# A fourth summed pair in the last gate/up block of a Hymba layer, with down's first activations split in steps of their own and the weight buffers handed out otherwise

## The chip, the cores and the metric

The kernel runs on one core of a Trainium2 chip. The metric is device microseconds of one execution, taken as the median of several runs. A profile of one execution comes with it. In it PE is the matrix engine (TensorE), PEld its weight load, DVE the vector engine, ACT the scalar engine, POOL is GpSimd and SP the engine that here only issues DMAs. All times are in microseconds unless ns is written.

## What is computed

The reference is one decoder layer on 256 tokens with a model width of 2048, all of it in 32-bit floats:

```
u = rmsnorm(h) ; [lru_x|lru_gate|q|k|v|ret_gate] = u @ W_in      # 2048 -> 6144
a = rg_lru(causal_conv(lru_x)) * gelu(lru_gate)                  # gated linear recurrence
b = groupnorm(retention(rope(q), rope(k), v)) * silu(ret_gate)   # 8 heads of 128, chunks of 128
h = h + concat(a, b) @ W_out                                     # 2048 -> 2048
t = rmsnorm(h) ; h = h + (silu(t @ W_gate) * (t @ W_up)) @ W_down  # 2048 -> 5632 -> 2048
out = rmsnorm(h)
```

Nearly all the work is in the products with W_in, W_out, W_gate, W_up and W_down.

## The kernel before

**Three products for one.** The matrix engine multiplies in a rounded 32-bit format (fp32r). Every operand is therefore kept as a rounded high part and a low rest, made by `split`: ACT casts the high part (line 123) and DVE subtracts it from the source (line 124). One product of two blocks is three matmuls, high by high, high by low and low by high (`three`, lines 683 to 685).

**Path of a weight.** SP issues a DMA of 128 x 1024 floats (512 KB) into a `raw` buffer, ACT casts it into a `wh` tile, DVE subtracts into a `wl` tile, and PE reads both. There are 6 raw buffers (`rpool`) and 4 pairs of split tiles (`wpool`). From block 3 on, where the tiles of the mixer are no longer needed, `swap` opens two pools more: 2 raw buffers (`raw2`) and 2 pairs of split tiles (`split2`), and every fourth raw tile and every third split tile comes from them. `stop_more` ends that before block 12, and `swap_back`, after block 12, closes the two pools and puts in their place the tiles of the end: the residual `htok` (8 DMAs of 256 KB on POOL's queue) and the final norm's weights `fw` (4 more of 256 KB).

**Blocks and steps.** After the mixer the program consists of blocks: 0 and 1 (W_out), 2 to 12 (gate and up, 512 columns of each in a block, `NB` = 11) and two passes of down (`down_block`). A block goes through 8 pairs of 128-row slices of its weights (2 x 2 blocks of 128 x 512 for one pair). A plain pair takes 8 products, which are 24 matmuls. A summed pair takes 7, by sums of weight blocks and of activation blocks, which are 21 matmuls; for it DVE makes 4 sums of 128 x 512 (`add`, line 661), more pieces are split, and the second half of the weights is loaded a second time. A summed pair is worked off in two places: 4 of its products in the block before its own (`share`, class `Shared`), the other 3 in its own (`direct`, class `Direct`, with the second load). `SUMMED` says which pairs of a block are summed, and `STEPS` writes a block's steps as letters: p a plain pair, h half of one, s a share of the next block's summed pair, d a direct step. Blocks 4 to 10 have the steps `psdhsdhsdhsdhp`. The last three shares, in block 12, are those of down's first three pairs.

**Order.** A list of entries (weights to load, function to run) is walked in order; at each entry the loads are issued 3 ahead of need (`AHEAD`), and `tick` runs what was put off by `defer`. The framework's scheduler then sets the order of instructions on each engine, and adds the waits between engines and for free buffers.

**Other names that the change touches.** `sumsq` (line 291) collects the sum of squares of x for the first norm: ACT squares (line 308), POOL adds seven times (line 310) and folds once (line 311), and PE sums over the partitions (`rms_scale`, line 271). `make_left(p)` splits activation tile `ff[p]` for down, with its sums. `ft` (line 865) are the transposes of a gate/up block's result and `ff` (line 867) ACT's copies of them out of PSUM. `cr` and `sr` are tables for the rotation.

Of the kernel before, what the change touches and what calls it, by code (L numbers as in the profile page):

```python
# [8 lines left out]
F32 = mybir.dt.float32  # L9
# [5 lines left out]
P = 128  # L15
D = 2048
S = 256
# [14 lines left out]
SUMMED = ((), (4, 5), (2, 3), (1, 2, 3)) + ((0, 1, 2, 3),) * 8 + ((1, 2, 3),)  # L32
# [3 lines left out]
STEPS = ("pppspppspp", "ppspdpsdpp", "pdpsdpspspp", "pspsdpsdpsdp") + ("psdhsdhsdhsdhp",) * 7 + ("psdpsdpsddp", "psdpsdpsdpp")  # L36


EARLY_DOWN = (0, 1, 2)
SUMMED_DOWN = (9, 12, 15, 17, 19), (5, 7, 9, 11, 13, 15, 17)  # L40
# [4 lines left out]
def tile_hymba_layer(ctx: ExitStack, tc: tile.TileContext, A: dict, out: bass.AP):  # L45
# [5 lines left out]
    rpool = ctx.enter_context(tc.tile_pool(name="raw", bufs=6))  # L51
# [5 lines left out]
    late, resid, more, turn_of = [], [xpool], [], [0, 0]  # L57
# [16 lines left out]
    def split_tiles():  # L74
        turn_of[1] += 1
        pool_ = more[1] if more and turn_of[1] % 3 == 0 else wpool
        return [pool_.tile([P, 1024], F32R, tag=g, name=nm(g)) for g in ("wh", "wl")]

    def raw_tile():
        turn_of[0] += 1  # L80
        pool_ = more[0] if more and turn_of[0] % 4 == 0 else rpool
        return pool_.tile([P, 1024], F32, tag="raw", name=nm("raw"))
# [76 lines left out]
    program = []  # L159
# [131 lines left out]
    sumsq = cpool.tile([P, 512], F32, name="sumsq")  # L291
# [148 lines left out]
    cr = cpool.tile([P, S], F32, name="cr")  # L440
    sr = cpool.tile([P, S], F32, name="sr")
# [15 lines left out]
    half = {}  # L457
# [159 lines left out]
    class Quad:  # L617
# [5 lines left out]
        def __init__(self, src, sums, before=None):  # L623
            self.src, self.sums, self.before = src, sums, before
            self.parts = {}
            self.apart = False
# [12 lines left out]
        def load(self, half):  # L639
            r = raw_tile()  # L640
            nc.sync.dma_start(out=r, in_=self.src[:, half * 1024 : half * 1024 + 1024])
            if half == 0 and self.before:
                self.before()
            if not self.sums:
                self.cut(("b22", "b21") if half else ("b11", "b12"), r)
                return
            if half == 0:
                self.ra = r
                self.parts["b11"] = act_tile("bh", F32R), act_tile("bl", F32R)
                split(*self.parts["b11"], r[:, :512])  # L650
                return
            self.cut(("b22", "b21"), r)
            self.add(r)
            self.cut(("t1", "t3"), self.ra)
            self.cut(("t2", "t4"), r)
# [31 lines left out]
    def block(index, quads, lefts, post, ps, tail, early={}, ordered=False):  # L687
# [39 lines left out]
        for i in range(n):  # L727
            program.append(([quads[i]], step(i)))

# [30 lines left out]
    class Direct(Quad):  # L760
# [8 lines left out]
        def load(self, half):  # L769
            r = raw_tile()  # L770
            nc.sync.dma_start(out=r, in_=self.src[:, 1024:2048])
            self.cut(("b22", "b21"), r)
            self.parts["t4"] = self.shared.parts["t4"]
# [12 lines left out]
    class Block:  # L786
# [45 lines left out]
        def put(self, after):  # L832
            plain = [i for i in PLAIN[self.index] if i not in self.summed]
            for k, kind in enumerate(self.steps):
                if kind == "p":
                    i, n = plain.pop(0), len(plain)
                    quad = Quad(self.src(i), False)
                    run = lambda i=i, quad=quad, k=k, n=n: self.plain(i, quad, k == 0, n == 0)
# [12 lines left out]
                else:  # L851
                    m = self.steps[:k].count("s")
                    quad = after.shared[m]
                    run = lambda m=m: after.share(m)
                program.append(([quad], run))
# [258 lines left out]

    blocks = [Block(d, lambda i, d=d: A["w_out"][8 * d + i], y, out_post(d), STEPS[d], SUMMED[d]) for d in range(2)]
    blocks += [
# [4 lines left out]
    for b, after in zip(blocks, blocks[1:] + [down]):  # L1121
        if b.index == 3:
            program.append(([], swap))
        if b.index == NB + 1:
            program.append(([], stop_more))
        b.put(after)
    program.append(([], swap_back))
# [120 lines left out]
```

## Time and profile before

| | |
|---|---|
| runs, median (lowest to highest) | 1082.09 us (1081.95 to 1083.99) |
| profiled execution | 1082.46 us, of which the span is 1080.7 us |
| PE busy | 1070.2 us, 99% of the span |
| DVE, ACT, POOL busy | 964.1 us (89%), 664.5 us (61%), 57.2 us (5%) |
| granted TensorE clock | 0.998 of full |
| read from HBM | 239.46 MB, 225 GB/s over the span with what is written |

The busy shares stand per engine over the whole span. The chain of work that ended last is followed back from the last instruction, each piece to what released it; it is PE for 98%, and 22% each is one of the three lines of `three`. A view of waits lists, for an engine, how long it sat idle just before instructions of a line, and what ended that.

### The profile page before, as it was taken

How to read it: one execution, taken by the hardware profiler on the slowest of the kernel's cores; microseconds unless marked ns; L12 is line 12 of the kernel's file. 1: busy time of each engine (PE TensorE's matmuls, PEld its weight loads, DVE VectorE, ACT ScalarE, POOL GpSimd, SP SyncE). 2: the span in 40 equal slices, each digit the busy share in tenths (PEclk: the TensorE clock that was granted, in tenths of full speed). 3: DMA queues.
4: the chain of work that ended last, by engine and by line, in shares of the span. 5: the costliest groups of instructions: out<-in, count | busy, mean ns of one | idle time of the engine just before them, and what ended most of it. 6: DMA issues, size and time to landing. Idle time of an engine off the chain costs nothing.

```text
span 1080.7 us, 14590 instructions
## 1 busy us (share of the span) xinstructions
PE 1070.2 (99%) x5089; PEld 897.7 (83%) x5089; DVE 964.1 (89%) x1399; ACT 664.5 (61%) x947; POOL 57.2 (5%) x73
## 2 busy tenths in 40 slices
PE   9999999999999999999999999999999999999997
PEld 7888888888888888888888888888888888888886
DVE  7889789988878889989999999999999889997886
ACT  7666644468756676656656565665656656654563
POOL 0602230000000000000000000000002000000001
PEclk9999999999999999999999999999999999999999
DMA  9965475554556588677776777777767856474662
GB/s 325 336 213 171 159 254 166 183 176 158 192 195 234 183 304 273 231 235 256 257 270 228 251 260 242 263 269 232 258 234 270 289 181 214 162 245 159 214 212 101
DMA packets 71386, 244.62 MB, mean 226 GB/s; under 512 B 8208, under 2 KB 8592, under 8 KB 71312
## 3 DMA queue, kind: packets, MB, share of 16 engines
q1 hardware_dynamic: 68400, 236.34, 64.6%
q0 software_dynamic: 1472, 4.72, 1.3%
q10 hardware_dynamic: 1440, 2.62, 0.6%
q8 instruction: 40, 0.66, 0.2%
q14 instruction: 34, 0.28, 0.1%
HBM read 239.46 MB, written 4.19 MB: 225 GB/s over the span
## 4 chain that ended last, share of the span: by engine, by line
PE 98%; DVE 1%; DMA 1%; POOL 0%; SPq 0%; ACT 0%; issue 0%; POOLq 0%; ACTq 0%
PE c L685 22%; PE c L683 22%; PE c L684 22%; PE fm L194 11%; PE fm L196 5%; PE tm L174 3%; PE tm L175 3%; PE tm L176 3%; PE p L683 1%; PE p L685 1%; PE p L684 1%; PE ft L865 1%; DMA x<-in_x 1%; PE ht L588 0%; PE sc L492 0%; DVE wl L124 0%
## 5 line engine op out<-in xcount | busy, mean ns | idle before, releaser
L123 ACT CAST wh<-raw 128x1024 fp32r<-128x1024 f32 (+1 forms) x498 | 462.9, 959 | 323.8 <-PE c L685 130.8
L124 DVE TENSOR_TENSOR wl<-raw,wh 128x1024 fp32r<-128x1024 f32 (+1 forms) x498 | 542.2, 1115 | 72.5 <-ACT wh L123 71.2
L684 PE MATMUL c<-wl,ah 128*128 128x512 f32 x826 | 322.7, 391 | 0.0
L685 PE MATMUL c<-wh,al 128*128 128x512 f32 x826 | 321.8, 390 | 0.0
L683 PE MATMUL c<-wh,ah 128*128 128x512 f32 x826 | 280.3, 391 | 0.0
L683 PEld LDWEIGHTS c<-wh,ah 128*128 128x128 f32 x826 | 155.1, 188 | 32.0 <-ACT wh L123 0.3
L685 PEld LDWEIGHTS c<-wh,al 128*128 128x128 f32 x826 | 155.2, 188 | 31.8
L684 PEld LDWEIGHTS c<-wl,ah 128*128 128x128 f32 x826 | 155.2, 188 | 31.6
L194 PE MATMUL fm<-u,wh 128*128 128x512 f32 x512 | 161.4, 396 | 0.0
L196 PEld LDWEIGHTS fm<-u,wl 128*128 128x128 f32 x512 | 96.1, 188 | 22.4
L196 PE MATMUL fm<-u,wl 128*128 128x256 f32 x512 | 101.2, 279 | 0.0
L661 DVE TENSOR_TENSOR raw<-raw,raw 128x512 f32<-128x512 f32 x114 | 78.4, 689 | 2.0
L661 DVE TENSOR_TENSOR raw<-raw 128x512 f32<-128x512 f32 x114 | 78.3, 688 | 1.4
L194 PEld LDWEIGHTS fm<-u,wh 128*128 128x128 f32 x512 | 78.4, 189 | 0.3
L684 PE MATMUL c<-wl,sh 128*128 128x512 f32 x192 | 74.3, 390 | 0.0
L685 PE MATMUL c<-wh,sl 128*128 128x512 f32 x192 | 73.7, 390 | 0.0
L683 PE MATMUL c<-wh,sh 128*128 128x512 f32 x192 | 67.3, 391 | 0.3 <-ACT sh L123 0.3
L176 PE MATMUL tm<-wh,u 128*128 128x512 f32 x128 | 48.7, 391 | 0.0
L175 PE MATMUL tm<-wl,u 128*128 128x512 f32 x128 | 48.7, 393 | 0.0
L174 PE MATMUL tm<-wh,u 128*128 128x512 f32 x128 | 46.9, 394 | 1.4 <-ACT u L298 1.4
L683 PEld LDWEIGHTS c<-wh,sh 128*128 128x128 f32 x192 | 36.1, 188 | 8.1 <-ACT sh L123 0.7
L685 PEld LDWEIGHTS c<-wh,sl 128*128 128x128 f32 x192 | 36.1, 188 | 7.5
(247 smaller groups left out, 1027.4 us busy)
## 6 DMA issues: line engine op xcount, KB each, us to landing
raw<-in_w_gu SPq DMA_DIRECT2D x216, 512.0 KB, 5.3
raw<-in_w_down SPq DMA_DIRECT2D x91, 512.0 KB, 4.6
raw<-in_w_out SPq DMA_DIRECT2D x34, 512.0 KB, 3.7
raw<-in_w_lx SPq DMA_DIRECT2D x16, 512.0 KB, 6.4
raw<-in_w_k SPq DMA_DIRECT2D x16, 512.0 KB, 3.6
raw<-in_w_q SPq DMA_DIRECT2D x16, 512.0 KB, 4.2
raw<-in_w_rg SPq DMA_DIRECT2D x16, 512.0 KB, 3.5
raw<-in_w_lg SPq DMA_DIRECT2D x16, 512.0 KB, 3.5
```

Of the source, the lines that this page charges most:

```text
L123: act.copy(out=dst_h, in_=src)
L124: v.tensor_tensor(out=dst_l, in0=src, in1=dst_h.bitcast(F32), op=ALU.subtract)
L174: pe.matmul(ps, ah, wh, start=first, stop=False)
L175: pe.matmul(ps, ah, wl, start=False, stop=False)
L176: pe.matmul(ps, al, wh, start=False, stop=last)
L194: pe.matmul(ps, wh, hl, start=n + i == 0, stop=False)
L196: pe.matmul(ps[:, :S], wl, hl[:, :S], start=False, stop=n + i == len(order) - 1)
L661: v.tensor_tensor(out=dst, in0=a, in1=b, op=ALU.add)
L683: pe.matmul(p, ah, bh, start=first, stop=False, skip_group_check=onto)
L684: pe.matmul(p, ah, bl, start=False, stop=False, skip_group_check=onto)
L685: pe.matmul(p, al, bh, start=False, stop=last, skip_group_check=onto)
L865: pe.transpose(pt[:, o : o + P], g[:, (2 * b + c) * P : (2 * b + c) * P + P], ident)
```

## The change

The last gate/up block, 12, sums four pairs instead of three, so block 11 has a fourth share, and takes the steps of blocks 4 to 10; block 12 has a fourth direct step and one plain pair fewer. The splits of down's first four activation tiles become entries of their own ahead of steps 0, 2, 4 and 6 of block 12 (`ASIDE`). There are 7 raw buffers instead of 6. The 2 extra raw buffers are no longer handed out by turn, but by kind: to the loads of direct steps, and to the second half of a block's last plain pair (`brief`). The extra pools stay open into the first pass of down: `stop_more` runs after its step 9 and `swap_back` after its step 12 (`hooks`). `sumsq`, `cr` and `sr` move from the pool of constants to the pool of activation tiles.

```diff
-SUMMED = ((), (4, 5), (2, 3), (1, 2, 3)) + ((0, 1, 2, 3),) * 8 + ((1, 2, 3),)
+SUMMED = ((), (4, 5), (2, 3), (1, 2, 3)) + ((0, 1, 2, 3),) * 9
-STEPS = (...) + ("psdhsdhsdhsdhp",) * 7 + ("psdpsdpsddp", "psdpsdpsdpp")
+STEPS = (...) + ("psdhsdhsdhsdhp",) * 8 + ("psdpsdpsddp",)
+ASIDE = {(12, 0): 1, (12, 2): 2, (12, 4): 3, (12, 6): 4}
-    rpool = ctx.enter_context(tc.tile_pool(name="raw", bufs=6))
+    rpool = ctx.enter_context(tc.tile_pool(name="raw", bufs=7))
-    def raw_tile():
-        turn_of[0] += 1
-        pool_ = more[0] if more and turn_of[0] % 4 == 0 else rpool
+    def raw_tile(brief=False):
+        pool_ = more[0] if more and brief else rpool
-    sumsq = cpool.tile([P, 512], F32, name="sumsq")
+    sumsq = act_tile("sumsq")
-    cr = cpool.tile([P, S], F32, name="cr")
-    sr = cpool.tile([P, S], F32, name="sr")
+    turned = act_tile("turned")
+    cr, sr = turned[:, :S], turned[:, S:]
...
         def load(self, half):          # Quad
-            r = raw_tile()
+            r = raw_tile(self.brief and half == 1)
...
         for i in range(n):             # block
             program.append(([quads[i]], step(i)))
+            if i in hooks[ordered]:
+                program.append(([], hooks[ordered][i]))
...
         def load(self, half):          # Direct
-            r = raw_tile()
+            r = raw_tile(True)
...
                     quad = Quad(self.src(i), False)     # put
+                    quad.brief = n == 0
...
+                if (self.index, k) in ASIDE:
+                    program.append(([], lambda i=ASIDE[self.index, k]: make_left(i)))
                 program.append(([quad], run))
...
+    hooks = {0: {9: stop_more, 12: swap_back}, 1: {}}
...
-        if b.index == NB + 1:
-            program.append(([], stop_more))
         b.put(after)
-    program.append(([], swap_back))
```

**Order on ACT near the start.** The square into `sumsq` before, among the first activations (`u` are the normed inputs, `wh` high parts of weights):

```order
L298 ACTIVATE u_136<-x_82,small 128x256
L123 CAST wh_127<-raw_126 128x512
L298 ACTIVATE u_141<-x_82,small 128x256
L308 ACTIVATE sumsq<-x_82 128x512
L123 CAST wh_145<-raw_144 128x512
L298 ACTIVATE u_152<-x_83,small 128x256
```

And ACT before, some thirty instructions further on, where the other squares begin (`v` are copies out of PSUM):

```order
L123 CAST wh_337<-raw_336 128x1024
L123 CAST wh_343<-raw_342 128x1024
L1036 COPY v_360<-tm_208 128x512
L1036 COPY v_374<-tm_209 128x512
L308 ACTIVATE sq_378<-x_83 128x512
L308 ACTIVATE sq_381<-x_84 128x512
```

The same place on ACT in the changed kernel:

```order
L123 CAST wh_336<-raw_335 128x1024
L123 CAST wh_342<-raw_341 128x1024
L1041 COPY v_359<-tm_207 128x512
L1041 COPY v_373<-tm_208 128x512
L308 ACTIVATE sumsq_111<-x_82 128x512
L308 ACTIVATE sq_377<-x_83 128x512
L308 ACTIVATE sq_380<-x_84 128x512
```

The square into `sumsq` has moved from the first activations to just ahead of the seven others.

**Order on PE at the first norm.** The matmuls of the mixer's projections (`fm`) around the norm's (`rms`), before:

```order
L194 MATMUL fm_526<-u_263,wh_470 128x512
L196 MATMUL fm_526<-u_258,wl_471 128x256
L196 MATMUL fm_526<-u_263,wl_471 128x256
L194 MATMUL fm_526<-u_298,wh_470 128x512
L271 MATMUL rms_543<-ones,sumsq 128x2 x2
L194 MATMUL fm_526<-u_303,wh_470 128x512
```

And in the changed kernel:

```order
L194 MATMUL fm_525<-u_262,wh_469 128x512
L196 MATMUL fm_525<-u_257,wl_470 128x256
L196 MATMUL fm_525<-u_262,wl_470 128x256
L271 MATMUL rms_542<-ones,sumsq_111 128x2 x2
L194 MATMUL fm_525<-u_297,wh_469 128x512
L194 MATMUL fm_525<-u_302,wh_469 128x512
```

The norm's matmuls stand one matmul earlier.

**Order on ACT in block 12**, around the first copies of `ft` there (`ff`; `gated` is the gate's activation, `sh` and `ah` high parts of activations, `t4h` one of a summed weight). Before:

```order
L123 CAST t4h_7854<-raw_7842 128x512
L123 CAST wh_7904<-raw_7902 128x1024
L123 CAST wh_7910<-raw_7908 128x1024
L123 CAST wh_7945<-raw_7930 128x512
L867 COPY ff_7881<-ft_7876 128x512
L867 COPY ff_7888<-ft_7883 128x512
L123 CAST ah_7932<-ff_4531 128x512
```

And in the changed kernel:

```order
L123 CAST sh_7884<-s_7879 128x512
L123 CAST wh_7991<-raw_8004 128x512
L123 CAST t4h_7900<-raw_7888 128x512
L123 CAST wh_8080<-raw_8078 128x512
L872 COPY ff_7927<-ft_7922 128x512
L872 COPY ff_7934<-ft_7929 128x512
L123 CAST ah_7976<-ff_4917 128x512
```

In both a cast into a split tile stands ahead of the copies; in the changed kernel that tile, `wh_8080`, comes free with a matmul that stands 7 matmuls ahead of the first one that needs the PSUM bank which the copy empties.

## Rows read from the trace of the kernel before

**Rows 1.** Page, busy time of each engine, share of the span, instructions

```profile
PE 1070.2 (99%) x5089; PEld 897.7 (83%) x5089; DVE 964.1 (89%) x1399; ACT 664.5 (61%) x947; POOL 57.2 (5%) x73
```

**Rows 2.** Waits of PE: line, what released it, total us, times, longest

```profile
PE tm L174 <- ACT u L298: 1.4, 2, 1.0
PE warm L116 <- DVE eps_t L109: 1.1, 1, 1.1
PE c L683 <- ACT sh L123: 0.3, 1, 0.3
```

**Rows 3.** Chain in order of time: start, us, what

```profile
1051.04 0.91 PE c L683 x4
```

**Rows 4.** Windows: stretch, busy of PE, PEld, DVE, ACT, POOL; clock, DMA share, GB/s

```profile
700.00:760.00 60.00, 60.00 (x271) 49.73 (x270) 56.76 (x72) 37.38 (x49) 0.00 (x0) 1.00 0.75 252
780.00:840.00 60.00, 60.00 (x270) 49.76 (x269) 55.00 (x78) 37.74 (x50) 6.39 (x12) 1.00 0.74 254
```

**Rows 5.** Groups of 760 to 870, DVE: busy, mean ns of one, idle before

```profile
L661 DVE TENSOR_TENSOR raw<-raw,raw 128x512 f32<-128x512 f32 x12 | 8.3, 688 | 0.2
```

**Rows 6.** The same stretch, ACT

```profile
L123 ACT CAST wh<-raw 128x512 fp32r<-128x512 f32 x12 | 7.4, 618 | 1.6 <-PE c L685 1.5
```

**Rows 7.** Timeline of ACT: start, us, instruction, [idle before, releaser]

```profile
6.81 0.62 ACT L308 ACTIVATE sumsq<-x 128x512 f32<-128x512 f32 x1
8.43 0.62 ACT L123 CAST wh<-raw 128x512 fp32r<-128x512 f32 x1 [1.00 <-DMA raw<-in_w_v]
...
29.74 3.76 ACT L308 ACTIVATE sq<-x 128x512 f32<-128x512 f32 x7
33.40 1.99 ACT L123 CAST wh<-raw 128x1024 fp32r<-128x1024 f32 x2
```

**Rows 8.** Timeline of POOL

```profile
30.47 12.58 POOL L310 TENSOR_TENSOR sumsq<-sumsq,sq 128x512 f32<-128x512 f32 x7 [29.59 <-ACT sq L308]
43.13 1.60 POOL L311 TENSOR_TENSOR sumsq<-sumsq 128x256 f32<-128x256 f32 x1
```

**Rows 9.** Timeline of PE at the first norm

```profile
44.85 0.40 PE L194 MATMUL fm<-u,wh 128*128 128x512 f32 x1
45.08 0.50 PE L271 MATMUL rms<-ones,sumsq 128*128 128x2 f32 x4
```

**Rows 10.** Line 310 on POOL: duration ns least/median/most, first and last start

```profile
L310 POOL TENSOR_TENSOR sumsq<-sumsq,sq x7: 1287/1627/2270, 30.5 to 41.4; 128x512 f32<-128x512 f32 x7
```

**Rows 11.** Groups of DVE in 34.4 to 46, while POOL adds

```profile
L124 DVE TENSOR_TENSOR wl<-raw,wh 128x1024 fp32r<-128x1024 f32 x6 | 10.8, 1858 | 4.3 <-ACT wh L123 4.3
```

**Rows 12.** The same group in 48.5 to 70

```profile
L124 DVE TENSOR_TENSOR wl<-raw,wh 128x1024 fp32r<-128x1024 f32 x8 | 9.8, 1221 | 3.2 <-ACT wh L123 3.2
```

**Rows 13.** Timeline of PE in block 3

```profile
370.74 0.40 PE L683 MATMUL c<-wh,sh 128*128 128x512 f32 x1
371.43 0.50 PE L683 MATMUL c<-wh,sh 128*128 128x512 f32 x1 [0.30 <-ACT sh L123]
```

**Rows 14.** Timeline of ACT in block 12, the copies of `ft`

```profile
818.14 1.08 ACT L867 COPY ff<-ft 128x512 f32<-128x512 f32 x2 [1.55 <-PE ft L865]
```

**Rows 15.** Timeline of PE: first use of the PSUM bank that those copies empty

```profile
823.05 0.39 PE L683 MATMUL c<-wh,sh 128*128 128x512 f32 x1
```

**Rows 16.** DMA issues of 820 to 840: KB each, median us to landing

```profile
raw<-in_w_gu SPq DMA_DIRECT2D x5, 512.0 KB, 9.2
...
htok<-kept_rows POOLq DMA_DIRECT2D x8, 256.0 KB, 8.1
```

**Rows 17.** DMA issues of 870 to 890

```profile
raw<-in_w_down SPq DMA_DIRECT2D x7, 512.0 KB, 4.1
```

**Rows 18.** Waits of ACT in 820 to 845

```profile
ACT wh L123 <- DMA raw<-in_w_gu: 1.1, 3, 0.5
```

**Rows 19.** Waits of ACT in 870 to 960, the longest two

```profile
ACT wh L123 <- PE c L685: 14.0, 10, 1.9
ACT wh L123 <- DVE raw L661: 8.5, 4, 3.6
```

More of the change, by code (lines that the diff above doesn't have):

```diff
@@ L28 @@
 N_SMALL = 104
-SUMMED = ((), (4, 5), (2, 3), (1, 2, 3)) + ((0, 1, 2, 3),) * 8 + ((1, 2, 3),)
+SUMMED = ((), (4, 5), (2, 3), (1, 2, 3)) + ((0, 1, 2, 3),) * 9
 SUMMED_OUT, SUMMED_FFN = (4, 5), (0, 1, 2, 3)
 PLAIN = ((4, 5, 6, 7, 0, 1, 2, 3),) * 2 + (tuple(range(8)),) * 11
-STEPS = ("pppspppspp", "ppspdpsdpp", "pdpsdpspspp", "pspsdpsdpsdp") + ("psdhsdhsdhsdhp",) * 7 + ("psdpsdpsddp", "psdpsdpsdpp")
+STEPS = ("pppspppspp", "ppspdpsdpp", "pdpsdpspspp", "pspsdpsdpsdp") + ("psdhsdhsdhsdhp",) * 8 + ("psdpsdpsddp",)
 EARLY_DOWN = (0, 1, 2)
+ASIDE = {(12, 0): 1, (12, 2): 2, (12, 4): 3, (12, 6): 4}
 SUMMED_DOWN = (9, 12, 15, 17, 19), (5, 7, 9, 11, 13, 15, 17)
@@ L56, in tile_hymba_layer @@
     tpool = early.enter_context(tc.tile_pool(name="tmp", bufs=6))
-    late, resid, more, turn_of = [], [xpool], [], [0, 0]
+    late, resid, more, turn_of = [], [xpool], [], [0]
     extra = ExitStack()
@@ L74, in split_tiles @@
     def split_tiles():
-        turn_of[1] += 1
-        pool_ = more[1] if more and turn_of[1] % 3 == 0 else wpool
+        turn_of[0] += 1
+        pool_ = more[1] if more and turn_of[0] % 3 == 0 else wpool
         return [pool_.tile([P, 1024], F32R, tag=g, name=nm(g)) for g in ("wh", "wl")]
-    def raw_tile():
-        turn_of[0] += 1
-        pool_ = more[0] if more and turn_of[0] % 4 == 0 else rpool
+    def raw_tile(brief=False):
+        pool_ = more[0] if more and brief else rpool
         return pool_.tile([P, 1024], F32, tag="raw", name=nm("raw"))
@@ L625, in __init__ @@
             self.parts = {}
-            self.apart = False
+            self.apart = self.brief = False
         def cut(self, names, raw):
```

## Prediction

> **What bounds the kernel now.** I read the busy times first: PE is busy for 1070.2 of the span's 1080.7 us, DVE for 89%, ACT for 61%, POOL for 5% [rows 1]. A busy share alone is no proof of a bound, so PE's waits come next. There are three in the whole execution: 1.4 us for the first activations at the start, 1.1 us before the warm-up matmul, and 0.3 us in one place of block 3 [rows 2]. The 1.1 us lie before the first weights have come and are not touched. Around the wait of 0.3 us two matmuls start 0.69 us apart [rows 13], where their usual distance is 0.23 us: four high-by-high matmuls in a row take 0.91 us of the chain, 0.227 us each [rows 3]. So that place holds about 0.46 us of idle time, and the start 1.4 us. Nothing else does: in the windows of blocks 9 to 12 PE is busy in every microsecond at the full clock [rows 4].
>
> The kernel is therefore bound by the number of matmuls times 0.227 us. An edit to the feeding engines gives nothing by itself; it can only cost, by making PE wait. What is to be counted is matmuls, and then, one place after another, whether a result still comes in time.
>
> **The fourth pair.** One more summed pair has 21 matmuls rather than 24: three fewer. They all stand on PE's path, so 3 x 0.227 = 0.68 us go [rows 3]. This is the only gain of the whole change, because it is the only edit that takes work from PE.
>
> Its price on the other engines: four sums and three more subtractions of 128 x 512 on DVE, at 0.69 us each 7 x 0.69 = 4.8 us [rows 5]; three casts on ACT at 0.62 us, 1.9 us [rows 6]; one weight load of 512 KB. Do they stay covered? Block 11 takes the steps of blocks 4 to 10. In 700 to 760, in blocks with these steps, DVE works 56.8 of 60 us and PE doesn't wait; in 780 to 840, DVE works 55.0 of 60 [rows 4]. With all 4.8 us in the latter it would be 59.8 of 60, just full. But the sums belong to block 11's fourth share, and part of the later split work to block 12, so they spread over more than 60 us. I take no cost, and for the range the bound that one split tile is late by one DVE instruction, 0.69 us. If the cover went altogether, the 4.8 us less the 5.0 idle would still be nothing; DVE has to be late locally for a loss. ACT has 22 of 60 us idle there [rows 4].
>
> **Splits as steps of their own, and the copies behind a cast.** Down's first splits move, and no work is added by that. Yet ACT's order changes around the first copies of `ft` in block 12. A cast into a split tile stands ahead of them, and waits until PE frees that tile; the first matmul that needs the PSUM bank emptied by the copy is only 7 matmuls later, 7 x 0.227 = 1.59 us. In that time must fit: the end of the freeing matmul 0.39 us after its start [rows 15], the cast 0.62 us [rows 6], the copy 1.08/2 = 0.54 us [rows 14], together 1.55 us, and the signals between the engines, about 0.1 us by my guess. That is 1.65 against 1.59: a stall of 0.05 us. Before, the copies began at 818.14 us and PE needed the bank at 823.05 [rows 14, 15], over four microseconds later. Bounds: 0, if cast and copy overlap a little, and 0.7 us if the cast is one instruction late.
>
> **The square that moved.** Before, ACT squared into `sumsq` at 6.81 us, ahead of a cast that had to wait another 1.00 us for its weights [rows 7]. It cost nothing there, so taking it away gains nothing. Now it stands just ahead of the seven other squares. These took 3.66 us from the first start to the next cast's (29.74 to 33.40), 0.52 us each [rows 7]. All of ACT's later work there, and through it the DVE subtractions, comes 0.52 us later; and so does POOL's chain of adds, which waited for the first square and then ran without a gap until its fold ended at 43.13 + 1.60 = 44.73 us [rows 8]. Who waits for it? PE's matmuls of the norm, at 45.08 us, 0.35 us after the fold [rows 9]; and by the new order these stand one matmul earlier, where PE is at 44.85 us. The fold now ends at 44.73 + 0.52 = 45.25 us, so PE stands for 0.40 us, and with the signal I take 0.45 us. The cover that goes is exactly that slack of 0.35 us. Behind the norm's matmuls on PE queue all projections that follow, so the stall is lost for good. Bounds: 0, if the square overlaps the chain's start better than the order says; and more, if an add of POOL that ran by itself now meets a DVE subtraction. Such a meeting can be priced: the adds take 1.29 us at the least and 2.27 us at the most [rows 10], 0.98 us between them, while DVE's subtraction of 128 x 1024 takes 1.86 us in that stretch and 1.22 us after it [rows 11, 12]. One more meeting gives 0.45 + 0.98 = 1.43 us. I take 0.45 us, since the casts that release the subtractions move by the same 0.52 us as the adds, so that both keep their places to one another.
>
> By the Trainium skill ("GPSIMD Engine Reference", section "8. Key points") GpSimd shares its SBUF interfaces with VectorE and contends with its instructions that have two SBUF inputs. The trace agrees with that by the slower adds and subtractions just named. By the rule every add beside a subtraction is a slow one, so the delay would be 0.52 us only as long as their number stays; the other outcome is the second rival below.
>
> **Buffers.** The seventh raw buffer and the handing out by kind change when SP can issue, not what PE does. Where PE never waits for a weight, an earlier load is worth nothing. I cost it at nothing.
>
> **Extra buffers kept into down.** The 12 reloads on POOL's queue (3 MB) leave block 12, where eight of them are issued in 820 to 840 us [rows 16], and by the order of the program go to about 885 to 912 us. In 820 to 840 the weight loads took 9.2 us to land, against 4.1 us in 870 to 890 [rows 16, 17], and ACT waited for weights three times, 1.1 us in all [rows 18]; PE did not wait even then. So the collision leaves a place where it cost nothing on PE and goes to one where ACT waits only for buffers and sums, 14.0 and 8.5 us [rows 19]. By the same order their first use is some 35 us later still. I cost it at nothing, with the first rival as the bound.
>
> **Sum.** -0.68 + 0.45 + 0.05 = -0.18 us. The profiled execution took 1082.46 us (span 1080.70 and 1.76 around it); it becomes 1082.28. The median of the runs is 1082.09, 0.37 lower; it becomes **1081.9 us**, a ratio of 0.9998.
>
> **Rivals.**
>
> *Slower: the reloads starve down.* In down's first pass the weights come three loads ahead. A load feeds 12 matmuls or so, 2.7 us, so three give 8.2 us; a cast and a subtraction, 1.00 (half of 1.99) and 1.22 us [rows 7, 12], leave 6.0 us for the landing. It decides from a landing later than that. At the 9.2 us of rows 16 one load would be 3.2 us late: 1081.9 + 3.2 = 1085.1 us. For it: down's first pass is where ACT and DVE have the most to do between a landing and its use in a summed pair. Against it: with 9.2 us before, PE didn't wait either [rows 2, 16], so the eight buffers in fact give a longer lead, and now there are nine. Chance 0.07.
>
> By the Trainium skill ("DMA: Bandwidth & Descriptors", section "Issuing engines are not separate DMA queues") the DMAs that different engines start run on the same 16 DMA engines and interleave. The longer landings beside POOL's reloads agree with it, 9.2 against 4.1 us; it is what would make this rival come true.
>
> *The norm waits longer.* One add more beside a subtraction: -0.68 + 1.43 + 0.05 = +0.8, 1082.9 us. For it the 0.98 us between the fastest and the slowest add [rows 10]; against it the common shift. Chance 0.12.
>
> *Less stands than I think.* The norm's matmuls find the fold ready and the 0.46 us in block 3 vanish with other buffers: -0.68 - 0.46 = -1.14, 1080.9 us. Against it: the orders of all engines in block 3 stay, and PE waits there for a cast of an activation, not for a weight [rows 2, 13]. Chance 0.12.
>
> *The change does not do what it says.* Then the three matmuls stay and 1082.1 + 0.5 = 1082.6 us result. The order shows PE with three matmuls fewer, so I give it 0.01.
>
> *A second slow place.* DVE too full in block 11 or 12, two or three splits late by 0.69 us: +1.4 to 2.1, 1083.3 to 1084.0 us. Chance 0.06. Some place that I have not seen, gaining over 2.2 us: 0.03; the idle time of PE is too little for more.
>
> **Numbers.** The forecast has 0.59. A measurement tells about 0.2%, 2.16 us, from no change. Faster by that is only the unseen place, 0.03. Slower are the starved down and a part of the second slow place, 0.08. The rest is within, 0.89. The range takes in the forecast, both small rivals and the lower part of the second slow place: 1080.7 to 1083.4 us, which leaves about 0.15 out.
>
> **What the profile after would show.** PE with three matmuls of 128 x 512 fewer, still at 0.227 us each; DVE busy for about 4.8 us more, ACT for 1.9 us more. In PE's waits a new row, the norm's matmul waiting for POOL's line 311, 0.3 to 0.5 us; the waits of the first activations and of block 3 as they were; perhaps a row of the share in block 12 behind ACT's copy, under 0.1 us. The reloads of `htok` land in 885 to 912 us with weight landings near 9 us, and no wait of PE for a cast there. The prediction is wrong if PE waits for casts or subtractions in 774 to 960 us for more than a microsecond, or if the matmuls' distance is not 0.227 us.

## The result, and the profile after

The changed kernel is slower, by a little: median 1084.57 us (1083.43 to 1086.0) against 1082.93 us for the kernel before (1081.8 to 1083.99), 13 runs each; ratio 1.0017, 95% interval 1.001 to 1.0025. Forecast were 1081.9 us and a range from 1080.7 to 1083.4 us. The 1.64 us of loss lie inside the 0.2% that were named as the limit of no change, but the time lies outside the range, and the sign of the loss is clear. The forecast started from 1082.09 us, the median of three runs; the 13 runs here have 1082.93 for the same kernel, 0.84 us more. That is a third of the distance to the forecast and no fault of its terms. But on the old base, too, the time would be 1082.09 + 1.64 = 1083.73 us, above the range.

Its profiled execution took 1084.57 us with a span of 1082.80, 2.09 us above the span of before. The page answers [rows 1]:

```profile
PE 1071.6 (99%) x5086; PEld 896.3 (83%) x5086; DVE 968.3 (89%) x1406; ACT 665.6 (61%) x950; POOL 55.8 (5%) x73
```

The counted work is as forecast: three matmuls fewer on PE, seven instructions more on DVE and three more on ACT. Their price is smaller than forecast, 4.2 us on DVE instead of 4.8, 1.1 us on ACT instead of 1.9. What is new stands in PE's waits (line, releaser, total us, times, longest), to be read against [rows 2]:

```profile
PE tm L174 <- ACT u L298: 1.1, 3, 0.6
PE warm L116 <- DVE eps_t L109: 1.1, 1, 1.1
PE c L683 <- ACT c L811: 0.5, 1, 0.5
PE c L683 <- ACT wh L123: 0.4, 2, 0.2
PE c L683 <- ACT sh L123: 0.3, 1, 0.3
```

The first two and the last were there before. Two rows are new: one wait for ACT's copy of `q` back to PSUM, two for casts of weights. Idle time near a matmul is longer than the part that is put down to a wait. So I measured the loss by the lateness of PE: by how much the same matmul starts later than in the trace of before, counted from the first matmul up to block 10 and from the last one in down. Besides the start, this lateness grows at three places only, and is flat between them:

| stage | lateness gained, us |
|---|---|
| start (to 13 us) | +0.16 |
| first norm (45 to 46 us) | +0.31 |
| from there to 763 us | 0.00 |
| blocks 11 and 12 (to 871 us) | +0.22, in spite of 0.68 less work |
| down's first pass (to 985 us) | 0.00 |
| down's second pass | +1.44 |

Together 2.13 us. The start moves in both directions from execution to execution (-0.90 to +0.23 in the table below), with the landing of the first inputs; I don't count it.

**The norm.** POOL and PE, to be read against [rows 8, 9]:

```profile
30.95 13.11 POOL L310 TENSOR_TENSOR sumsq<-sumsq,sq 128x512 f32<-128x512 f32 x7 [30.07 <-ACT sq L308]
44.14 1.07 POOL L311 TENSOR_TENSOR sumsq<-sumsq 128x256 f32<-128x256 f32 x1
```

```profile
44.77 0.39 PE L196 MATMUL fm<-u,wl 128*128 128x256 f32 x2
45.26 0.61 PE L271 MATMUL rms<-ones,sumsq 128*128 128x2 f32 x4
```

POOL's fold ends at 44.14 + 1.07 = 45.21 us, 0.48 later than before (0.16 of it is the later start of the whole execution), and PE's norm starts 0.05 us after it. Before, 0.35 us lay between the two. I take it that PE waits for POOL there, although no row of PE's waits says so; e5 and e6 below test it.

**Block 12.** PE, DVE and ACT around the wait for the copy of `q` (start, us, instruction):

```profile
852.71 0.39 PE L683 MATMUL c<-wh,ah 128*128 128x512 f32 x1
853.57 0.50 PE L683 MATMUL c<-wh,ah 128*128 128x512 f32 x1 [0.47 <-ACT c L811]
```

```profile
849.34 0.69 DVE L809 TENSOR_TENSOR p<-c,p 128x512 f32<-128x512 f32 x1
849.94 2.35 DVE L124 TENSOR_TENSOR wl<-raw,wh 128x1024 fp32r<-128x1024 f32 x2
852.21 0.68 DVE L810 TENSOR_TENSOR q<-p,c 128x512 f32<-128x512 f32 x1
```

```profile
846.38 0.58 ACT L808 COPY p<-c 128x512 f32<-128x512 f32 x1
...
851.93 1.04 ACT L123 CAST wh<-raw 128x1024 fp32r<-128x1024 f32 x1
852.92 0.59 ACT L811 COPY c<-q 128x512 f32<-128x512 f32 x1
```

Two matmuls start 0.86 us apart where 0.23 is usual. ACT's copy begins at 852.92, when `q` is just ready (852.21 + 0.68 = 852.89). `q` is late because DVE took `p` at 849.34 only, though ACT had delivered its input at 846.96: DVE worked off splits in between. But ACT is no earlier: the cast ahead of the copy in its queue runs from 851.93 to 852.97. Both queues reach the copy at the same moment, so an earlier `q` alone would not have helped. The windows of the ten microseconds ahead (columns as in [rows 4]), before and after:

```profile
840.00:850.00 10.00, 10.00 (x45) 8.28 (x45) 9.37 (x12) 6.73 (x10) 0.00 (x0) 1.00 1.02 372
```

```profile
840.00:850.00 10.00, 10.00 (x46) 8.27 (x45) 10.00 (x14) 9.04 (x14) 0.00 (x0) 1.00 0.78 253
```

DVE has no idle time left there, and ACT's work rises from 6.73 to 9.04 us. A full window alone proves nothing: DVE works 10.00 us in 800 to 810 as well, and PE doesn't wait there. Here the late `p` and `q` show that work has queued up.

**Down's second pass.** PE, ACT and DVE of the changed kernel at the first of three such places (`bh` and `bl` are the high and low part of a piece of a summed pair's first half):

```profile
1020.06 0.39 PE L685 MATMUL p<-wh,sl 128*128 128x512 f32 x1
1020.47 0.50 PE L683 MATMUL p<-wh,sh 128*128 128x512 f32 x1
1020.80 0.40 PE L683 MATMUL c<-wh,ah 128*128 128x512 f32 x1
1021.41 0.96 PE L683 MATMUL c<-wh,ah 128*128 128x512 f32 x3 [0.21 <-ACT wh L123]
```

```profile
1012.98 0.62 ACT L123 CAST bh<-raw 128x512 fp32r<-128x512 f32 x1 [3.63 <-DMA raw<-in_w_down]
1013.51 2.00 ACT L123 CAST wh<-raw 128x1024 fp32r<-128x1024 f32 x2
1019.36 3.90 ACT L123 CAST wh<-raw 128x1024 fp32r<-128x1024 f32 x4 [3.86 <-DVE raw L661]
```

```profile
1013.63 0.69 DVE L124 TENSOR_TENSOR bl<-raw,bh 128x512 fp32r<-128x512 f32 x1 [3.03 <-ACT bh L123]
1014.36 0.69 DVE L661 TENSOR_TENSOR raw<-raw 128x512 f32<-128x512 f32 x1
...
1017.84 0.68 DVE L661 TENSOR_TENSOR raw<-raw,raw 128x512 f32<-128x512 f32 x1
1018.56 0.69 DVE L661 TENSOR_TENSOR raw<-raw 128x512 f32<-128x512 f32 x1
```

And ACT of the kernel before at the same step:

```profile
1016.27 0.62 ACT L123 CAST bh<-raw 128x512 fp32r<-128x512 f32 x1 [4.21 <-DMA raw<-in_w_down]
1016.79 3.89 ACT L123 CAST wh<-raw 128x1024 fp32r<-128x1024 f32 x4
1021.20 1.05 ACT L123 CAST wh<-raw 128x1024 fp32r<-128x1024 f32 x1 [0.51 <-PE c L685]
```

And DVE of the kernel before:

```profile
1016.92 0.69 DVE L124 TENSOR_TENSOR bl<-raw,bh 128x512 fp32r<-128x512 f32 x1 [1.44 <-ACT bh L123]
1017.65 0.69 DVE L661 TENSOR_TENSOR raw<-raw 128x512 f32<-128x512 f32 x1
...
1019.39 0.68 DVE L661 TENSOR_TENSOR raw<-raw,raw 128x512 f32<-128x512 f32 x1
...
1023.52 0.69 DVE L661 TENSOR_TENSOR raw<-raw,raw 128x512 f32<-128x512 f32 x1
...
1025.26 0.69 DVE L661 TENSOR_TENSOR raw<-raw 128x512 f32<-128x512 f32 x1
```

In both kernels ACT comes to the cast `bh` of a summed pair's first half before that half has landed, and waits; everything behind it in ACT's queue, and through `bl` in DVE's, waits too. Before, that was the only long wait of a period: right behind it ACT had four casts to do. Of a period's four sums of line 661, DVE made two behind `bl` and two well ahead of the next `bl`. After, all four stand behind `bl` (between 1014.36 and 1019.25 us). The four casts wait for the last of them, and ACT waits a second time, 3.86 us. PE then gets its weights too late; the lateness grows by 0.80 us here, by 0.51 near 1032 and by 0.13 near 1043 us. So ACT and DVE work in another order in this pass than before, and no edit of the change speaks of that. The waits of ACT in 1005 to 1041, before and after:

```profile
ACT bh L123 <- DMA raw<-in_w_down: 15.9, 4, 4.2
ACT wh L123 <- PE c L685: 1.3, 2, 0.8
```

```profile
ACT wh L123 <- DVE raw L661: 11.2, 4, 3.9
ACT bh L123 <- DMA raw<-in_w_down: 8.1, 3, 3.6
```

The 11.2 us for line 661 don't exist before in this stretch. They are the mark by which I look for this loss below.

### The profile page after: what moved, and what is told of

It reads as the page before. It is cut to its first block, busy times and chain, and to the rows that moved or that the text cites. A ratio compares the mean times of both kernels' runs of the same rounds, so it can differ in the third digit from the quotient of the medians.

```text
span 1082.8 us, 14600 instructions
## 1 busy us (share of the span) xinstructions
PE 1071.6 (99%) x5086; PEld 896.3 (83%) x5086; DVE 968.3 (89%) x1406; ACT 665.6 (61%) x950; POOL 55.8 (5%) x73
## 4 chain that ended last, share of the span: by engine, by line
PE 91%; DVE 3%; POOL 1%; issue 1%; DMA 1%; ACT 1%; SPq 0%; POOLq 0%; ACTq 0%
PE c L683 21%; PE c L685 21%; PE c L684 21%; PE fm L194 10%; PE fm L196 5%; PE tm L175 2%; PE tm L176 2%; PE tm L174 2%; DVE wl L124 1%; POOL sumsq L310 1%; PE p L685 1%; PE p L684 1%; PE p L683 1%; PE ft L870 1%; DMA raw<-in_w_lx 1%
## 5 line engine op out<-in xcount | busy, mean ns | idle before, releaser
L685 PE MATMUL c<-wh,al 128*128 128x512 f32 x820 | 318.6, 389 | 0.0
L176 PE MATMUL tm<-wh,u 128*128 128x512 f32 x128 | 48.5, 390 | 0.0
```

The source lines that it names most:

```text
L176: pe.matmul(ps, al, wh, start=False, stop=last)
L685: pe.matmul(p, al, bh, start=False, stop=last, skip_group_check=onto)
```

## The experiments

The theory after the result: the norm's loss comes from the moved square; the second pass's from the seventh raw buffer, because of which the framework's scheduler lays out ACT and DVE in another order; the wait in block 12 from DVE being full, by the fourth pair or by the splits in steps of their own. All kernels compute the whole layer. The lateness by stage is that of each profiled execution against the one of before; the ratio is against runs of the kernel before in the same series.

| run | ratio (95%) | start | norm | blocks 11, 12 | first pass | second pass |
|---|---|---|---|---|---|---|
| changed | 1.0017 (1.001 to 1.0025) | +0.16 | +0.31 | +0.22 | 0.00 | +1.44 |
| e9 changed again | 1.0013 (1.0004 to 1.0022) | -0.42 | +0.31 | +0.26 | 0.00 | +1.19 |
| e1 changed, 6 raw | 1.0009 (1.0 to 1.0017) | +0.04 | +0.31 | +0.26 | 0.00 | 0.00 |
| e2 before, 7 raw | 1.0011 (1.0002 to 1.002) | -0.15 | +0.29 | 0.00 | 0.00 | +1.43 |
| e3 no steps of their own | 1.0064 (1.0051 to 1.0077) | -0.44 | +0.30 | +6.74 | 0.00 | +0.90 |
| e4 extra closed as before | 1.0011 (1.0002 to 1.002) | -0.26 | +0.31 | +0.61 | +0.03 | +1.29 |
| e5 before, moved square | 1.0003 (0.9994 to 1.0012) | -0.90 | +0.33 | 0.00 | 0.00 | +0.06 |
| e6 square back, 6 raw | 0.9999 (0.999 to 1.0008) | -0.59 | 0.00 | +0.26 | 0.00 | +0.54 |
| e7 e6, last split later | 1.0013 (1.0004 to 1.0022) | -0.12 | 0.00 | +3.74 | 0.00 | +1.25 |
| e8 before, fourth pair | 1.0017 (1.0008 to 1.0026) | -0.59 | +0.02 | +1.47 | +0.89 | 0.00 |
| e10 changed, three pairs | 1.0012 (1.0003 to 1.002) | -0.58 | +0.29 | +0.06 | 0.00 | +1.38 |
| e11 e6, splits in block 11 | 1.0024 (1.0014 to 1.0034) | +0.23 | +0.01 | +2.69 | 0.00 | +0.55 |
| e12 e6, all in block 11 | 1.0031 (1.0019 to 1.0042) | -0.69 | +0.17 | +3.41 | 0.00 | +0.57 |

Between 200 and 763 us the lateness stays within 0.01 us, but for +0.91 in e6 (at 381 us, block 3), +0.13 in e7 and +0.36 in e12. A median scatters by about a microsecond, so single losses are read from the stages, and the ratios only as their sum.

**e1, six raw buffers in the changed kernel.**

```
-    rpool = ctx.enter_context(tc.tile_pool(name="raw", bufs=7))
+    rpool = ctx.enter_context(tc.tile_pool(name="raw", bufs=6))
```

> The changed kernel with 6 raw buffers instead of 7 (8 with the two extra ones), nothing else. Against the kernel before, the changed kernel's matmuls run later by 0.47 us after the first norm, by 0.69 us from 871 to 1007 us and by 2.13 us from 1041 us on; so the second pass of down loses 1.43 us, in three waits at 1020 to 1032 us. Theory: that loss comes from the seventh raw buffer, with which ACT and DVE take the first half of the next summed pair ahead of the sums and casts of the one at hand. Then it goes here: no wait of PE after 1000 us, and the time is 1.4 us below the changed kernel's 1084.6, about 1083.1 us. Rival: it comes from the reloads and the extra buffers that now reach into down, or from the lateness left by block 12; then the waits at 1020 to 1032 us stay, and the time is about 1084.6 us.

The second pass loses nothing. ACT's waits in 1005 to 1041 are those of before again, with no row for line 661:

```profile
ACT bh L123 <- DMA raw<-in_w_down: 15.7, 4, 4.2
ACT wh L123 <- PE c L685: 1.2, 2, 0.7
```

The profiled execution is 1.5 us below the changed kernel's; the median, 1084.01, only 0.6, within the scatter of both. The profiled execution is also the fastest of its eleven, and six of them took 1084.0 to 1085.0 us; what those six lost, no trace shows. Reloads and buffers that reach into down are in this kernel, so the rival falls.

**e2, seven raw buffers in the kernel before**, with the room made as the change does.

```
-    rpool = ctx.enter_context(tc.tile_pool(name="raw", bufs=6))
+    rpool = ctx.enter_context(tc.tile_pool(name="raw", bufs=7))
...
-    sumsq = cpool.tile([P, 512], F32, name="sumsq")
+    sumsq = act_tile("sumsq")
...
-    cr = cpool.tile([P, S], F32, name="cr")
-    sr = cpool.tile([P, S], F32, name="sr")
+    turned = act_tile("turned")
+    cr, sr = turned[:, :S], turned[:, S:]
```

> The kernel before with 7 raw buffers, and with sumsq, cr and sr taken from the activation tiles, which makes the room for it; nothing else of the change. Theory of the seventh buffer: the second pass of down loses 1.4 us here as well, and start and first norm 0.47 us: about 1084.8 us, with PE's waits for casts near 1020 to 1032 us. Rival (reloads in down, or block 12's lateness): only the 0.47 us, about 1083.4 us, and no wait of PE after 1000 us.

The other direction gives the same: +1.43 us in the second pass, +0.29 at the norm, nothing else, and the mark:

```profile
ACT wh L123 <- DVE raw L661: 11.2, 4, 3.9
ACT bh L123 <- DMA raw<-in_w_down: 8.1, 3, 3.9
```

The runs show less than the traces. By the ratios, seven buffers cost 0.0004 to 0.0008 in the changed kernel (1.0017 and 1.0013 against 1.0009) and 0.0008 in the kernel before (1.0011 against 1.0003 in e5), which is 0.4 to 0.9 us, and no such difference is clear of its intervals. The 1.43 us are what the order costs in the profiled executions.

In the programs, the order of ACT and DVE through most of the second pass is that of the kernel before in e1, e5, e6, e7, e11 and e12, all with 6 raw buffers, and that of the changed kernel in e2, e3 and e10, all with 7. Only e8 (6) and e4 (7) have orders of their own. In all six executions with seven buffers ACT waits 8.3 us or more for line 661 in 1008 to 1043 us, and 0.90 to 1.44 us are lost in the pass. In those with six there is no such wait in that stretch, but for 2.9 us in e8, and no such loss.

**e3, no steps of their own; e4, extra buffers closed as before.**

```
-ASIDE = {(12, 0): 1, (12, 2): 2, (12, 4): 3, (12, 6): 4}
+ASIDE = {}
```

> The changed kernel without the steps of their own for down's first splits (they fall back into the steps that need them). In the changed kernel PE stands still for 0.6 us at 853.6 us, before the matmul that needs ACT's copy of q, and q came late from DVE, behind two splits of down's activations. Theory: these splits, put ahead, cause it; without them the wait goes, and the time falls by 0.6 us to about 1084.0 us. Rival: DVE is late there because of the fourth pair's sums and splits; then the wait stays at 0.5 us or more, and the time at about 1084.6 us. The second pass of down keeps its 1.4 us in both.

Both theories fell: the time rose by 5 us, and the second pass lost 0.90 us rather than 1.4. Without steps of their own the splits come all at the end of block 12, and PE waits for a cast of one (`ah`) and for the copy of `q`:

```profile
PE c L683 <- ACT ah L123: 2.4, 1, 2.4
PE c L683 <- ACT c L811: 1.4, 1, 1.4
```

So the steps of their own are not what harms; they keep a worse wait away. Part of the loss comes after the waits. PE's windows there:

```profile
855.20:860.40 5.20, 5.20 (x12) 4.13 (x13) 3.18 (x6) 0.00 (x0) 0.00 (x0) 0.50 0.62 245
860.50:865.00 4.50, 4.50 (x21) 3.69 (x20) 0.00 (x0) 0.88 (x1) 0.00 (x0) 1.00 0.00 0
```

Behind these standstills the granted clock was 0.50, the lower of the two levels, for twelve matmuls, 5.20/12 = 0.43 us each in place of 0.227: 2.5 us more. It had fallen already between the two waits: it is 1.00 in 853.0 to 853.5 and 0.50 in 853.6 to 855.1 us.

```
-    hooks = {0: {9: stop_more, 12: swap_back}, 1: {}}
+    hooks = {0: {}, 1: {}}
...
+        if b.index == NB + 1:
+            program.append(([], stop_more))
         b.put(after)
+    program.append(([], swap_back))
```

> The changed kernel with the extra buffers given up where the kernel before gives them up: before block 12, with the reloads right after it. Theory of the seventh buffer: the second pass of down still loses 1.4 us; the landings of weights at 820 to 840 us rise again to about 9 us; about 1084.6 us. Rival (reloads and extra buffers in down cause the second pass's loss): the loss goes, about 1083.1 us.

As the theory has it: the second pass still loses 1.29 us. Of its landings the expectation was wrong: weights took 5.4 and 6.9 us in 820 to 840, not 9. Blocks 11 and 12 lose 0.61 us rather than 0.22, so by this pair of executions keeping the extra buffers open through block 12 is worth some 0.4 us there.

**e5, only the moved square; e6, the square back and six raw buffers.** e5 is e2 with 6 raw buffers, e6 is e1 with `sumsq`, `cr` and `sr` from the pool of constants.

> The kernel before, with only sumsq, cr and sr taken from the activation tiles (6 raw buffers). In the changed kernel and in all experiments with the moved square so far, PE runs 0.3 us later after the first norm than ahead of it. Theory: the square that now stands ahead of the seven others makes POOL's adds end 0.52 us later, beyond PE's slack; then PE is 0.3 us later after the norm here too, nothing else is later, and the time is 0.3 us above the kernel before, about 1082.9 us. Rival: the 0.3 us come from the seventh buffer's weight loads beside the start's; then 0 here.

> The changed kernel with 6 raw buffers and with sumsq, cr and sr where the kernel before has them; the fourth pair, the steps of their own, the handing out by kind and the extra buffers into down stay. Theory: no loss at the norm and none in down's second pass; the wait of 0.6 us before the copy of q in block 12 stays; against the kernel before +0.9 in blocks 11 and 12, -0.7 for the matmuls: +0.2 us, about 1082.8 us. Rival: a loss has another cause than its named part and stays: +0.3 (norm) or +1.4 us (second pass) more.

The norm's loss follows the square: 0.29 to 0.33 us in all eight executions that have it moved with `sumsq` in an activation tile, 0.00 to 0.02 in four of the five without. In the fifth, e12 (0.17), the norm starts 0.05 us behind the fold as well: PE was 0.69 us ahead of the kernel before there, and POOL's adds only 0.34, so the slack was used up without the square. In e5 the fold ends at 44.15 us and the norm starts at 44.21, and the norm's loss stands alone but for 0.06 us (median 1082.94 against 1082.93, too small for the ratio). e6 stands level with the kernel before, 0.9999, as forecast. Against the changed kernel's 1.0017 that is 1.9 us, and the two intervals don't meet (that of e9 just does): what the square and the seventh buffer cost together is shown by the runs, too. But the stages are not as forecast: its profiled execution lost 0.91 us in block 3 and 0.54 at 1000 us. There ACT waited 3.0 us for the landing of a first half, against 2.1 before: one microsecond more, at a place where the order has none to spare, even with six buffers. e7, e11 and e12 lose 0.37 to 1.12 us at the same place, 1000 to 1004 us, behind waits of 2.9 to 3.7 us, and 0.14 to 0.19 us in the rest of the pass, where kernels with seven buffers lose theirs. In these four the load at 988 us (of the kernel before's time) took 5.4 to 6.0 us to land, against 4.6 before. e1, e5 and e8 lose nothing there.

**e7, e11, e12, the splits elsewhere.** All three are e6 with another line `ASIDE`:

```
 e7   ASIDE = {(12, 0): 1, (12, 2): 2, (12, 4): 3, (12, 8): 4}
 e11  ASIDE = {(11, 2): 1, (11, 3): 2, (11, 4): 3, (12, 0): 4}
 e12  ASIDE = {(11, 1): 1, (11, 2): 2, (11, 3): 3, (11, 4): 4}
```

> Like the run with the square back and 6 raw buffers, and with the fourth of the splits of their own put ahead of step 8 of block 12 instead of step 6, so that one subtraction of down's activations (0.6 us) leaves DVE's queue ahead of p and q. Theory: q, and ACT's copy of it, come 0.6 us earlier, PE's wait of 0.6 us at 853 us goes, and the time is about 0.45 us below the kernel before: 1082.1 us. Rival: DVE and ACT are late there as a whole, by the fourth pair's work; then a wait of 0.4 us or more stays or moves behind: about 1082.8 us.

DVE made `q` at 851.31 us, where e6 made it at 852.06 with PE 0.3 us later: it did come sooner. The copy didn't. ACT of e7:

```profile
851.78 1.05 ACT L123 CAST wh<-raw 128x1024 fp32r<-128x1024 f32 x1 [0.85 <-DMA raw<-in_w_down]
852.74 1.26 ACT L879 ACTIVATE gated<-c,r_tok 128x512 f32<-128x512 f32 x2
853.89 0.60 ACT L811 COPY c<-q 128x512 f32<-128x512 f32 x1
```

It stood behind a cast that waited for its weights and two activations, PE waited 2.4 us, and the clock fell to the lower level here too. In this execution ACT's queue held the copy, not DVE's. It is not a typical one: two of this kernel's twelve runs, this one among them, took 1087 us, the others 1083.2 to 1084.9, so most can't have lost 3.74 us here. How much of a wait they kept, no trace shows. The theory's 1082.1 us was reached by none.

> Like the run with the square back and 6 raw buffers, and with the splits of down's first activations put ahead of steps 2, 3 and 4 of block 11 and step 0 of block 12, where DVE had 2 us of 10 idle (780 to 790 us). On DVE no split of down's activations then stands in the dozen instructions ahead of p and q, and on ACT the copy of q follows one activation sooner. Theory (DVE full at 840 to 850 us): PE's wait at the copy of q goes, and the time is 0.4 to 0.6 us below the kernel before, about 1082.3 us. Rival: the wait moves to block 11 or to another place of block 12; then 0.2 us above the kernel before or more.

> The same with all four splits ahead of steps 1 to 4 of block 11. Theory: as with the run before it, no wait at the copy of q, about 1082.3 us. Rival: block 11, whose fourth share already fills DVE in 790 to 820 us, gets a wait of PE of its own, above 0.5 us.

Here the rivals hold. In e11 the wait in block 12 is gone, as the theory has it, but DVE is full earlier, and PE waits in block 11:

```profile
810.00:820.00 10.00, 8.77 (x38) 6.63 (x37) 10.00 (x15) 5.16 (x7) 0.00 (x0) 1.00 0.95 349
840.00:850.00 10.00, 10.00 (x45) 8.26 (x45) 7.59 (x9) 8.37 (x10) 0.00 (x0) 1.00 0.83 268
```

DVE had 2.4 us to spare in 840 to 850 then, none in 810 to 820, where PE stood still for 1.2 us, in part for block 11's own copy of `q`. e12 loses 3.41 us in the same way, with its longest waits in block 11 (0.7 us for a `wl`). In none of the three other arrangements that were tried did the splits come free.

**e8, only the fourth pair; e10, the change with three pairs.**

> The kernel before with only the fourth pair in block 12 (SUMMED and STEPS), without steps of their own for down's first splits. Theory: without these steps the splits of down's first activations pile up at block 12's end, as in the changed kernel without them, where PE lost 6.8 us there: some us lost in block 12, about 1087 us or more, with PE waiting for casts of activations; nothing lost in down's second pass. Rival: the fourth pair by itself is harmless, and the pile came only from the buffers kept open: three matmuls fewer, about 1081.9 us.

> The changed kernel with three summed pairs in block 12 as before; all else of the change stays. Theory: DVE, which works in every microsecond of 840 to 850 us with the fourth pair, has time there, so PE's wait at the copy of q goes; the norm's 0.3 us and the 1.4 us of down's second pass (seven raw buffers) stay: 1.7 us above the kernel before, about 1084.6 us. Rival: the splits in steps of their own or the buffers by kind make that wait; then it stays, 2.3 us above, about 1085.2 us.

e8's blocks 11 and 12 lose 1.47 us net, with PE waiting for DVE's `al` and ACT's `ah`, splits of down's activations:

```profile
PE c L685 <- DVE al L124: 1.0, 1, 1.0
PE c L683 <- ACT ah L123: 0.6, 1, 0.6
```

That is the pile that was expected, but smaller than the few microseconds of its expectation (three of the twelve runs took 1086.2 to 1087.0 us), and 0.89 us more are lost at 947 us. e10 takes the fourth pair out of the change, and the wait at the copy of `q` is gone: no such row, 0.06 us in blocks 11 and 12, the norm and the second pass unchanged. DVE in 840 to 850 there:

```profile
840.00:850.00 10.00, 10.00 (x46) 8.28 (x45) 9.75 (x12) 7.47 (x9) 0.00 (x0) 1.00 0.91 312
```

DVE is nearly as full, but it made `q` at 848.75, 3.5 us earlier than in the changed kernel. So the fourth pair brings that wait. By e10 and the changed kernel it costs 0.22 - 0.06 = 0.16 us in place of a gain of 0.68.

**e9, the changed kernel again.**

> The changed kernel once more, for a second profile. Theory: the places of PE's waits are set by the order of the instructions and return: 0.3 us at the norm, 0.6 us at the copy of q near 853 us, 1.3 to 1.5 us in down's second pass near 1020 to 1032 us; about 1084.5 us. Rival: they are chance of one execution and stand elsewhere or are missing.

The waits return at the same places: 0.31 us at the norm, 0.63 us before the matmul at 852.99, 1.19 us in the second pass. They are of the order, not of one execution.

No version is faster than the kernel before. The best, e6, is level with it.

## Why the prediction was wrong, point by point

- **PE bound, 0.227 us a matmul, three fewer: right.** It is worth 0.68 us, and no more.
- **The fourth pair's price: the step failed.** The sum has no term for it. "Do they stay covered?" was answered by a window that ends at 840 us and had 5 of 60 us to spare on DVE. The place that was late lies behind it: in 840 to 850 DVE had 0.63 us to spare before and none after, and ACT reached the copy of `q` no sooner than DVE made `q`. A mean over 60 us hides the ten in which a queue forms. The prediction had it as the rival of a second slow place (0.06, +1.4 to 2.1 us); it was the likelier case, with 0.63 us at the wait and 0.84 us in all (from -0.68 to +0.16, e10).
- **The first copies of `ft` behind a cast: right place, small as forecast.** Forecast 0.05 us (1.65 - 1.59 is 0.06); two matmuls there start 0.15 us later than usual in all. The guess of 0.1 us for the signals fits: 0.05 us pass from the fold to the norm's matmuls, 0.06 from the copy of `q` to its matmul. The copy that cost more was that one, some twenty microseconds on.
- **The moved square: right in mechanism, 0.45 us forecast, 0.31 measured** (0.29 to 0.33). Measured from PE, POOL's fold came 0.32 us later, not 0.52: in the trace of before, ACT's last cast ahead of the squares (27.84 us) came late with its weights and held them up; in the changed kernel ACT waits for PE there and reaches its squares 0.2 us sooner. That the adds and the subtractions "keep their places to one another" was wrong. One add more ran beside a subtraction, as the rival of the longer wait had it (13.11 us for the chain against 12.58, median add 2.16 us against 1.63 [rows 10]). But the fold was faster, 1.07 against 1.60 us, so that nothing was lost by it. It is not the square's doing: all six executions with seven buffers have a median add of 2.16 us and a fold of 1.06 to 1.07, all eight with six have 1.62 to 1.63 and 1.59 to 1.60, e1 and e5 with the moved square among them. With seven, DVE makes four `wl` ahead of another subtraction, `gl`, with six three. What the Trainium skill ("GPSIMD Engine Reference", section "8. Key points") says of GpSimd and VectorE sharing their interfaces agrees with the slower adds.
- **"Buffers ... I cost it at nothing": the step that failed most, 1.2 to 1.4 us.** The reasoning was that an earlier load is worth nothing where PE never waits for weights. That is true of the load. But the number of buffers also enters the scheduler's planning, and ACT and DVE came out in another order through the whole second pass of down. The prediction compared the orders at the start, at the norm and in block 12, and left out the second pass, since no edit touches it; the listing of the order shows the difference. Its sign of being wrong, more than a microsecond of waits in 774 to 960 us, did not look there either; the waits in that stretch stayed at 0.5 us.
- **The reloads in down: right, and too cautious.** No lateness in the first pass. Weights landed in 4.5 us in 885 to 915 us, not the 9 that were expected, `htok` in 5.4.
- **The sum.** Forecast -0.68 + 0.45 + 0.05 = -0.18 us. By stages of the profile: +0.31, +0.22 and +1.44, 1.97 us without the start (1.76 in e9); the medians of 13 runs say 1.64. The failed terms are the two that were put at nothing: the buffers (1.44 us) and the fourth pair's cover (0.84).

What stays open: how the scheduler comes to place the first half's split ahead of the sums with seven buffers was not looked into, only that it does, and that this order costs 1.2 to 1.4 us here. Nor was an order tried that uses seven buffers and keeps the sums ahead. Open too is why the load near 988 us lands late in e6, e7, e11 and e12 (four of four, so hardly by chance) and not in e1, which differs from e6 only in the place of `sumsq`, `cr` and `sr`; and why the runs show less of the seventh buffer's loss than the traces.

## What to carry to other kernels

When an engine's order is laid out by a scheduler, a buffer more or less is an edit to the order of the whole program behind it: compare the orders of every stage that uses the pool, above all those that no line of the diff touches. Judge whether an engine can take more work by windows about as long as the lead that its results have (here ten microseconds, not sixty). A full window is only a reason to look: 800 to 810 was full and cost nothing. So follow the last short chains at a block's end, such as `p`, `q` and the copy back, through both queues that they pass. A saving on the engine that sets the end is kept only if every helper is still in time at its tightest place.

## What the hardware showed that was not expected

A standstill of PE can cost more than its length. Two traces have a wait of 2.4 us, and in both the granted clock fell from 1.00 to 0.50, the lower of the two levels, 0.6 us after PE had gone on. In e3 it had fallen before the next wait, of 1.4 us; the twelve matmuls behind both took 0.43 us each, which added 2.5 us. In e7 it was 0.53 in the mean of the next 3.5 us. Waits of 0.7 us (e11) and of 0.6 and 1.0 us close together (e8) left it at 1.00.
